# The second norm's shift and scale: columns by one-column products, or by small SBUF-to-SBUF transfers and a sum

## The chip, the cores and the metric

One Trainium2 chip, one of its cores. The metric is device time in microseconds (us) of one launch, median of the runs shown.

## What is computed

One layer of a decoder trunk, 256 tokens of width 1024, float32. Cut to what matters:

```python
mod = silu(c) @ w_ada + b_ada                     # 6 vectors of 1024 from one condition vector
sh1, sc1, g1, sh2, sc2, g2 = split(mod, 6)
h = rms_norm(x, norm1_g) * (1 + sc1) + sh1
ca, cb, q, k, v, gate_conv, gate_attn = split(h @ w_in)
y_conv = conformer_conv(ca, cb, ...)              # 31-tap causal convolution, layer norm, silu, @ w_pw2
y_attn = diff_attention(q, k, v, ...)             # 8 heads, two maps each
merged = sigmoid(gate_conv) * y_conv + sigmoid(gate_attn) * y_attn
x = x + g1 * (merged @ w_out)
h2 = rms_norm(x, norm2_g) * (1 + sc2) + sh2       # sh2, sc2: the vectors of this change
x = x + g2 * moe_ffn(h2, ...)                     # 64 experts, top 8, and one shared
```

## The kernel before

The work has two halves. **The mixer** (to about 337 us): first the modulation of the first norm, then the products of h with w_in in fourteen chunks of 512 columns, two chunks of the convolution's w_pw2 (p0, p1) and two of w_out (o0, o1). Every product is three matmuls on a high and a low part: `splits` casts a weight tile on ACT (L795), `lo_part` subtracts on POOL or VectorE (L776), `products` issues the matmuls (L802 to L804 with tokens as rows, L811 to L813 with channels as rows; the p chunks take the latter, the o chunks the former). Beside this run the convolution `conv` on VectorE (DVE; L859 for the first tap, L863 for thirty more, for eight channel blocks), six units of attention `attn` (scores L1012 and mask L1016, reduce and scale L1023 to L1040, transposes L1046, value products L1057, sub-norm L1069 to L1084), and when the last convolution block is done `layer_norm` (L1102 to L1157), whose result the p products read. Then follow merge, o products, the second norm, routing and ranks. **The experts** (from about 358 us to the end) stream their weights from HBM and multiply.

The modulation's six vectors come in twelve halves of 512; the first four make the first norm's columns in another way. `ada(i)` makes half i for i = 4 to 11: 16 matmuls (L550, in `ada_mm`) leave in a PSUM bank four partial sums, each in 32 equal rows, and ACT copies the bank to a buffer `s` (L742, 128x512). For i = 4, 5, 10, 11 (g1, g2) a matmul with the selector `sel4` (L749) sums the four and spreads the result over all rows. For i = 6, 7 (sh2) and 8, 9 (sc2) the result is wanted as columns, 64 partitions by 8: element c*8+k of the half goes to partition c, column k. Eight products (L758) do that before the change: `s` is the stationary operand, one column of `sel4` the moving one. DVE adds the bias column from PSUM (L762 or L764), and for i = 8, 9 forms the scale (L766).

Nothing in the program text fixes the order of the engines' instructions. Each piece is a generator that announces an engine and a cost in us (`yield "P", 1.0`: 1.0 us of TensorE); the planner `Plan` (L40 to L167) plays all generators at build time, gives each engine to the candidate that can start first and, among those, to the one of highest priority (`PRIO`, L25: attention 8, layer norm 7.5, `ada` 2, the convolution 0), and issues instructions in the order found. A changed cost or step moves all that is planned after it. DMAs on the SP queue (weights) and on ACT's queue are ordered so too.

```python
yield "P", 1.0
for k in range(K):
    nc.tensor.matmul(p[h, k:k + 1], sv[:, k], sel4[:, 0:1], start=True, stop=True)
yield pl.ev("cols")
yield TS(8)
```

Of the kernel before, what the change touches and what calls it, by code (L numbers as in the profile page):

```python
# [14 lines left out]
OP = mybir.AluOpType  # L15
AX = mybir.AxisListType
# [159 lines left out]
def TS(n):  # L176
    return "D", 0.13 + 0.00052 * n
# [10 lines left out]
def AP(n, table=None):  # L188
    return "A", 0.06 + 0.00082 * n, table
# [6 lines left out]
def MM(n):  # L196
    return "P", n / 2400.0
# [3 lines left out]
def tile_hybrid_block(ctx, tc, x, c, positions, w_ada, b_ada, norm1_g, w_in, conv_dw, conv_dw_b,  # L201
# [3 lines left out]
    nc = tc.nc  # L205
    P, T, D, K = 128, 256, 1024, 8
# [6 lines left out]
    pl = Plan()  # L213
# [218 lines left out]
    def done(key, q, now=None):  # L432
        now = pl.cur.ready if now is None else now
        w = loaded[key]
        if w.off[q] in halves:
            e = halves.pop(w.off[q])
            load(*e, [1], now)
            advance(now)
        elif w.off[q] in once:
            once.remove(w.off[q])  # L440
        elif w.off[q] == LAST:
            w2s.close()
            obs = ctx.enter_context(tc.tile_pool(name="obs", bufs=1)).tile([P, 8 * KB], F32R, name="obs")
            pl.put("ob", *(ob_of(obs[:, i * D:(i + 1) * D]) for i in range(2)))
        else:
            pl.pools["w"].append((now, w.off[q]))
            advance(now)
# [17 lines left out]
    sel4 = cst.tile([P, P], F32, name="sel4")  # L465
# [44 lines left out]
    pcol = cst.tile([P, 96], F32, name="pcol")  # L510
    c2 = pcol[:, 65:89].rearrange("p (a k) -> p a k", a=3)
# [21 lines left out]
    for k in range(K):  # L533
        p = B[k // 2][:, (k % 2) * T:(k % 2 + 1) * T]
# [11 lines left out]
    def ada_mm(i, s):  # L546
        w = loaded["a", i].k
        for k in range(K):
            g = k % 4
            nc.tensor.matmul(s[32 * g:32 * g + 32], ccol[:, k:k + 1].to_broadcast([P, 32]), w[k],  # L550
                             start=(k < 4), stop=(k >= 4))
# [10 lines left out]
    h32 = cst.tile([P, 3, 256], F32, name="h32")  # L562
    pl.put("h32", *(h32[:, i] for i in range(3)))
    pl.put("sa", *sa)
    s8_ = cst.tile([P, 4, 3, 8], F32, name="s8")
    pl.put("s8", *(s8_[:, i] for i in range(4)))
    pl.put("t2", *(temp(2 * i, 512) for i in range(3)))
# [155 lines left out]
    p2 = cst.tile([P, K], F32, name="p2")  # L723
    a2c = cst.tile([P, K], F32, name="a2c")
    b2c = cst.tile([P, K], F32, name="b2c")

    def late_ada(i):
        yield from ada(i, "sa")

    def ada(i, pool):  # L730
        yield pl.ev("mod", 3)
        yield pl.ev("L", "a", i, 3)
        yield max(loaded["a", i].at)
        row = i in (4, 5, 10, 11)
        p = yield Get("bank")
        yield "P", 1.8
        ada_mm(i, p)
        for q in range(2):
            done(("a", i), q)
        s = yield Get(pool)  # L740
        yield AP(512)
        nc.scalar.copy(s, p)  # L742
        if row:
            r = brow[i]
            yield pl.ev("param", {4: 3, 5: 4, 10: 11, 11: 12}[i])
            yield "G", 1.25
            nc.gpsimd.tensor_tensor(s[r:r + 1], s[r:r + 1], badar[r:r + 1], op=OP.add)
            yield MM(4 * 512)
            nc.tensor.matmul(p, sel4, s, start=True, stop=True)  # L749
            d = slice((i % 2) * 512, (i % 2) * 512 + 512)  # L750
            yield AP(512)
            nc.scalar.copy((g1b if i < 10 else g2b)[:, d], p)
        else:
            h = slice(64 * (i % 2), 64 * (i % 2) + 64)
            sv = s.rearrange("p (c k) -> p k c", k=K)
            yield "P", 1.0
            for k in range(K):
                nc.tensor.matmul(p[h, k:k + 1], sv[:, k], sel4[:, 0:1], start=True, stop=True)  # L758
            yield pl.ev("cols")
            yield TS(8)  # L760
            if i < 8:
                nc.vector.tensor_tensor(b2c[h], p[h, 0:K], c2[h, 0], op=OP.add)  # L762
            else:
                nc.vector.tensor_tensor(p2[h], p[h, 0:K], c2[h, 1], op=OP.add)  # L764
                yield TS(8)
                nc.vector.scalar_tensor_tensor(a2c[h], p2[h], 1.0, c2[h, 2], op0=OP.add, op1=OP.mult)  # L766
        pl.put("bank", p)
        pl.put(pool, s)
        pl.set("ada", i)

# [1151 lines left out]
    for i in range(4, 10):  # L1922
        pl.spawn(ada(i, "sa"))
# [77 lines left out]
```

## Time and profile before

| | |
|---|---|
| median of 3 runs | 820.47 us (818.65 to 822.19) |
| the profiled execution | 819.49 us, span 817.7 us, mean granted TensorE clock 0.969 |
| busy share of the span | PE 94%, DVE 54%, ACT 40%, POOL 24% |
| HBM | 330 GB/s mean over the span, about 420 GB/s from 358 us on |

PE is TensorE, DVE is VectorE, ACT is ScalarE, POOL is GpSimd, SP is the engine that issues most DMAs; ACTq and POOLq are DMA issues of those engines. A float32 matmul is recorded as two, so that eight products show as 16 records. "PEclk" is the granted clock of TensorE: 1.00 is 2.4 GHz, 0.50 is 1.2 GHz. An [idle <-engine line] behind an instruction is time for which its engine stood idle before it, and what ended the wait.

### The profile page before, as it was taken

How to read it: one execution, taken by the hardware profiler on the slowest of the kernel's cores; microseconds unless marked ns; L12 is line 12 of the kernel's file. 1: busy time of each engine (PE TensorE's matmuls, PEld its weight loads, DVE VectorE, ACT ScalarE, POOL GpSimd, SP SyncE). 2: the span in 40 equal slices, each digit the busy share in tenths (PEclk: the TensorE clock that was granted, in tenths of full speed). 3: DMA queues.
4: the chain of work that ended last, by engine and by line, in shares of the span. 5: the costliest groups of instructions: out<-in, count | busy, mean ns of one | idle time of the engine just before them, and what ended most of it. 6: DMA issues, size and time to landing. Idle time of an engine off the chain costs nothing.

```text
span 817.7 us, 13180 instructions
## 1 busy us (share of the span) xinstructions
PE 766.1 (94%) x4759; PEld 469.8 (57%) x4759; DVE 444.6 (54%) x1035; ACT 324.9 (40%) x713; POOL 192.4 (24%) x246
## 2 busy tenths in 40 slices
PE   3999999899996999999999797999999999999997
PEld 2898777589784987545454141354464455444543
DVE  5458998999996677433433141344344344433443
ACT  4356656865759755223221021232232232232220
POOL 3003788888572693000002000000000000000000
PEclk9999999899997999989999898999999999999999
DMA  9998776546654676469999999999999999999993
GB/s 312 365 336 288 261 253 227 180 161 227 228 184 155 239 280 252 165 245 390 390 420 420 422 421 420 421 422 420 420 421 422 421 420 421 420 421 419 419 413 139
DMA packets 69883, 271.04 MB, mean 331 GB/s; under 512 B 6085, under 2 KB 15893, under 8 KB 46520
## 3 DMA queue, kind: packets, MB, share of 16 engines
q1 hardware_dynamic: 69464, 270.00, 84.9%
q8 instruction: 38, 0.62, 0.3%
q0 software_dynamic: 304, 0.16, 0.1%
q14 instruction: 29, 0.24, 0.1%
q10 hardware_dynamic: 48, 0.01, 0.0%
HBM read 269.11 MB, written 1.05 MB: 330 GB/s over the span
## 4 chain that ended last, share of the span: by engine, by line


## 5 line engine op out<-in xcount | busy, mean ns | idle before, releaser
L1802 PE MATMUL bank<-fa 128*32 128x512 f32 (+2 forms) x1048 | 203.7, 608 | 8.3 <-DMA fa<-in_w_exp_gu_dram 8.3
L1802 PEld LDWEIGHTS bank<-fa 128*32 128x32 f32 (+2 forms) x1048 | 60.3, 124 | 132.1 <-issue 107.3
L863 DVE SCALAR_TENSOR_TENSOR bank<-fa,tap,bank 128x256 f32<-128x256 f32 x232 | 112.9, 486 | 6.1
L1676 DVE SCALAR_TENSOR_TENSOR fa<-bank,gsc,h 128x256 f32<-128x256 f32 x28 | 13.5, 484 | 170.1 <-ACT h L1672 170.1
L1849 PE MATMUL bank<-fa 128*32 128x512 f32 (+1 forms) x496 | 83.9, 596 | 0.0
L1672 ACT ACTIVATE h<-bank 128x256 f32<-128x256 f32 x28 | 10.8, 385 | 179.7 <-PE bank L1802 179.7
L776 POOL TENSOR_TENSOR rb<-fa,rb 128x512 fp32r<-128x512 f32 x46 | 60.2, 1317 | 65.6 <-ACT rb L795 64.6
L1694 DVE TENSOR_TENSOR fa<-bank,fa 128x512 f32<-128x512 f32 x54 | 37.4, 692 | 65.5 <-PE bank L1849 62.7
L776 POOL TENSOR_TENSOR ra<-fa,ra 128x512 fp32r<-128x512 f32 x48 | 63.9, 1339 | 20.5 <-ACT ra L795 17.1
L1762 ACT CAST obs<-fa 128x512 fp32r<-128x512 f32 x54 | 33.4, 618 | 83.7 <-DVE fa L1694 83.7
L1719 DVE TENSOR_TENSOR fa<-fa,bank 128x512 f32<-128x512 f32 x108 | 66.7, 678 | 0.0
L1491 ACT ACTIVATE fa<-bank,b2c,a2c 128x256 f32<-128x256 f32 x108 | 53.6, 561 | 20.8 <-PE bank L1523 20.8
L795 ACT CAST ra<-fa 128x512 fp32r<-128x512 f32 x76 | 46.8, 622 | 37.0 <-PE bank L812 22.9
L1523 PE MATMUL bank<-ra 128*128 128x256 f32 x448 | 60.5, 288 | 0.0
L1710 PE MATMUL bank<-obs,ra 128*128 128x512 f32 x216 | 58.3, 412 | 0.0
L795 ACT CAST rb<-fa 128x512 fp32r<-128x512 f32 x68 | 42.0, 623 | 37.8 <-PE bank L812 22.4
L1802 PE MATMUL bank<-late_w,fa 128*32 128x512 f32 (+2 forms) x168 | 51.9, 627 | 4.1 <-DMA late_w<-in_w_exp_gu_dram 4.1
L1523 PEld LDWEIGHTS bank<-ra 128*128 128x128 f32 x448 | 55.6, 191 | 0.2
L1710 PEld LDWEIGHTS bank<-obs,ra 128*128 128x128 f32 x216 | 38.7, 188 | 28.8 <-issue 21.5
L811 PE MATMUL bank<-ra 128*128 128x256 f32 x160 | 47.8, 299 | 1.9 <-ACT ra L577 1.8
L1849 PEld LDWEIGHTS bank<-fa 128*32 128x32 f32 (+1 forms) x496 | 22.8, 119 | 41.1 <-issue 35.3
L811 PE MATMUL bank<-ra,rb 128*128 128x256 f32 x160 | 46.1, 288 | 0.0
(376 smaller groups left out, 1391.5 us busy)
## 6 DMA issues: line engine op xcount, KB each, us to landing
fa<-in_w_exp_gu_dram SPq DMA_DIRECT2D x100, 1024.0 KB, 19.8
fa<-in_w_exp_down_dram SPq DMA_DIRECT2D x50, 1024.0 KB, 19.8
fa<-in_w_ada_dram SPq DMA_DIRECT2D x24, 1024.0 KB, 7.9
fa<-in_w_in_dram SPq DMA_DIRECT2D x22, 1024.0 KB, 5.3
late_w<-in_w_exp_gu_dram SPq DMA_DIRECT2D x17, 1024.0 KB, 19.3
late_w<-in_w_exp_down_dram SPq DMA_DIRECT2D x12, 1024.0 KB, 6.8
fa<-in_w_exp_gu_dram SPq DMA_DIRECT2D x22, 512.0 KB, 9.4
fa<-in_w_in_dram SPq DMA_DIRECT2D x12, 512.0 KB, 9.4
```

Of the source, the lines that this page charges most:

```text
L776: (nc.gpsimd if e == "G" else nc.vector).tensor_tensor(hl[:, 1], w.k[k], hl[:, 0].bitcast(F32), op=OP.subtract)
L795: nc.scalar.copy(hl[:, 0], w.k[k])
L811: nc.tensor.matmul(o, hl[:, 0, mm], src_t[:, k, 0], start=(k == 0 and m % 2 == 0), stop=False)
L863: nc.vector.scalar_tensor_tensor(cv[:, m] if j == TAPS - 1 else acc, u_sb[:, m, j:j + T], tap[:, m, j:j + 1], acc, op0=OP.mult, op1=OP.add)
L1491: nc.scalar.activation(xt[:, k, 0:ns], p3[:, f2, 0:ns], AF.Identity, bias=b2c[:, k:k + 1], scale=a2c[:, k:k + 1])
L1523: nc.tensor.matmul(p3[:, f2, 0:ns], xr[:, a, t, (f + f2) * P:(f + f2 + 1) * P], tables[b0][:, t, 0:ns], start=(f2 + t + a == 0), stop=(f2 ...
L1694: nc.vector.tensor_tensor(o32, pd[h], g2b[:, h * 512:(h + 1) * 512], op=OP.mult)
L1710: nc.tensor.matmul(p, info.pT[:, t * P:(t + 1) * P], ob[a], start=(a == 0), stop=(a == 1))
L1719: nc.vector.tensor_tensor(x_sb[:, t, d], x_sb[:, t, d], p, op=OP.add)
L1762: nc.scalar.copy(ob[0], o32)
L1802: nc.tensor.matmul(pg[o:o + m], info.xt[:, k, o:o + m], loaded["g", js[e]].k[k], start=(k == 0), stop=(k == K - 1))
L1849: nc.tensor.matmul(pd[h][o:o + m], info.aT[:, f, o:o + m], loaded["d", js[e]].k[f][:, h * 512:(h + 1) * 512], start=(f == 0), stop=(f == 1))
```

## The change

For i = 6 to 9 the products go. Behind ACT's copy of the bank to `s` (L742 before, L744 after) the bank is given back at once; four DMAs from ACT's queue (after: L762) take row 32g of `s`, for g = 0 to 3, one row of 512, and lay each as 64 partitions by 8 into `parts`, a part of the tile `pcol`; DVE sums over the four (L767 TENSOR_REDUCE, 64x8 from 64x8x4), adds the bias (L770), and for i = 8, 9 forms the scale (L774). The plan counts 0.4 us of ACT for the four issues and lets the reduce start 3.0 us after them.

```diff
+    for i in range(2):
+        pl.put(f"acol{i}", pcol[64 * i:64 * i + 64, 0:32].rearrange("p (g k) -> p g k", g=4))
...
             h = slice(64 * (i % 2), 64 * (i % 2) + 64)
-            sv = s.rearrange("p (c k) -> p k c", k=K)
-            yield "P", 1.0
-            for k in range(K):
-                nc.tensor.matmul(p[h, k:k + 1], sv[:, k], sel4[:, 0:1], start=True, stop=True)
+            pl.put("bank", p)
+            p = None
+            parts = yield Get(f"acol{i % 2}")
+            yield "A", 0.4
+            for g in range(4):
+                nc.scalar.dma_start(parts[:, g], s[32 * g:32 * g + 1])
+            yield pl.cur.ready + 3.0
             yield pl.ev("cols")
+            yield TS(32)
+            half = b2c[h] if i < 8 else p2[h]
+            nc.vector.tensor_reduce(half, parts.rearrange("p g k -> p k g"), axis=AX.X, op=OP.add)
+            pl.put(f"acol{i % 2}", parts)
             yield TS(8)
-            if i < 8:
-                nc.vector.tensor_tensor(b2c[h], p[h, 0:K], c2[h, 0], op=OP.add)
-            else:
-                nc.vector.tensor_tensor(p2[h], p[h, 0:K], c2[h, 1], op=OP.add)
+            nc.vector.tensor_tensor(half, half, c2[h, 0 if i < 8 else 1], op=OP.add)
+            if i >= 8:
                 yield TS(8)
                 nc.vector.scalar_tensor_tensor(a2c[h], p2[h], 1.0, c2[h, 2], op0=OP.add, op1=OP.mult)
-        pl.put("bank", p)
+        if row:
+            pl.put("bank", p)
```

The instructions are re-planned between the first group of products (113 us in the trace of before) and the end of the p products (292 us); ahead of that and behind it the engines' orders are the same but for buffer numbers. SP's order of weight loads is the same throughout. In the listings below line numbers of after are those of before plus 2 (up to L744) or plus 8 (from L771 on).

First place, **ACT around the first group**, after, with the semaphores that an instruction waits for. A DMAHW semaphore is one of eight that the hardware DMAs of SP and ACT take in turn, and a DMA waits until the earlier DMA of its semaphore has landed:

```order
106 L918 ACTIVATE s_211<-s_211 128x8 [waits DVE_49]
107 L744 COPY fa<-bank_77 128x512 [waits PE_49]
108 L762 DMA pcol<-fa 64x1x8 [waits DMAHW2_49,Activation_49]
109 L762 DMA pcol<-fa 64x1x8 [waits DMAHW3_49]
110 L762 DMA pcol<-fa 64x1x8 [waits DMAHW4_49]
111 L762 DMA pcol<-fa 64x1x8 [waits DMAHW5_49]
112 L803 CAST rb<-fa 128x512 [waits PE_49,Pool_49]
113 L803 CAST ra<-fa 128x512 [waits PE_49,Pool_49]
```

Four issues stand ahead of casts that feed the products; before, the cast followed the copy directly.

Second place, **DVE at the end of the convolution** (L863 to fa is the last tap; L1110 and L1115 belong to the layer norm, the other lines to attention). Before:

```order
251 L1023 TENSOR_REDUCE mx<-bank_79 128x2
252 L1084 SCALAR_TENSOR_TENSOR fa<-bank_74,sl_213,fa 128x4x128
253 L863 SCALAR_TENSOR_TENSOR bank_77<-fa,tap,bank_77 128x256 x5
254 L863 SCALAR_TENSOR_TENSOR fa<-fa,tap,bank_77 128x256 x2
255 L1110 TENSOR_SCALAR fa<-bank_78 128x256
256 L1115 TENSOR_TENSOR fa<-fa 128x256 x5
257 L1023 TENSOR_REDUCE mx<-bank_74 128x2
258 L1031 RECIPROCAL mx<-mx 128x2x2
```

After:

```order
291 L871 SCALAR_TENSOR_TENSOR bank_74<-fa,tap,bank_74 128x256
292 L1092 SCALAR_TENSOR_TENSOR fa<-bank_75,sl_213,fa 128x2x128
293 L1079 TENSOR_SCALAR mx<-mx 128x2
294 L871 SCALAR_TENSOR_TENSOR bank_74<-fa,tap,bank_74 128x256 x2
295 L1083 TENSOR_TENSOR fa<-bank_75,mx 128x256
296 L871 SCALAR_TENSOR_TENSOR fa<-fa,tap,bank_74 128x256 x2
297 L1031 TENSOR_REDUCE mx<-bank_73 128x2
298 L1092 SCALAR_TENSOR_TENSOR fa<-bank_78,sl_213,fa 128x2x128
299 L1031 TENSOR_REDUCE mx<-bank_76 128x2
300 L1118 TENSOR_SCALAR fa<-bank_80 128x256
```

Attention work that stood behind the last tap has moved ahead of it.

Third place, **PE around the layer norm's last sum (L1138; after, L1146)**, up to the first p product (L819 after; before, three more L1012 and two masks L1016 come first). Before:

```order
1157 L749 MATMUL bank_80<-fa,sel_111 128x512
1158 L1057 MATMUL bank_76<-fa 128x128 x4
1159 L1138 MATMUL bank_78<-fa,ones 128x128 x2
1160 L1046 MATMUL bank_73<-ident,fa 128x128 x4
1161 L1079 MATMUL bank_76<-ident,fa 128x128 x2
1162 L1057 MATMUL bank_73<-fa 128x128 x4
1163 L1012 MATMUL bank_74<-fa 128x256
```

After:

```order
1167 L1136 MATMUL bank_80<-ones,fa 128x1 x2
1168 L1065 MATMUL bank_75<-fa 128x128 x4
1169 L1146 MATMUL bank_80<-fa,ones 128x128 x2
1170 L1087 MATMUL bank_75<-ident,fa 128x128 x2
1171 L819 MATMUL bank_77<-ra 128x256
```

L749, which belongs to the halves 10 and 11, and the attention matmuls behind L1138 but for one L1079 (after: L1087) stand further ahead; so do those that stood among the 192 p products (12 instructions of L1046, L1057 and L1079).

## Rows read from the trace of the kernel before

**Rows 1.** The page: the span, and the busy time of each engine with its share of the span and its instructions.

```profile
span 817.7 us, 13180 instructions
...
PE 766.1 (94%) x4759; PEld 469.8 (57%) x4759; DVE 444.6 (54%) x1035; ACT 324.9 (40%) x713; POOL 192.4 (24%) x246
```

**Rows 2.** Stretches of the span (start:end, length, busy us of PE, PEld, DVE, ACT, POOL each with its number of records, granted clock, DMA share, GB/s): from the first group of products to the end of the convolution, from there to the first p product, the p products, the experts.

```profile
112.00:243.00 131.00, 125.09 (x821) 103.26 (x822) 121.00 (x261) 85.82 (x210) 100.74 (x135) 0.95 0.63 216
243.00:266.00 23.00, 15.36 (x76) 9.57 (x75) 15.79 (x44) 20.30 (x52) 6.98 (x8) 0.78 0.39 139
266.00:292.00 26.00, 25.53 (x212) 25.18 (x211) 15.19 (x29) 18.08 (x39) 19.45 (x17) 1.00 0.65 220
...
358.00:793.00 435.00, 421.06 (x2540) 200.73 (x2538) 160.16 (x346) 110.67 (x237) 5.09 (x4) 0.98 1.01 417
```

**Rows 3.** The instructions of L758: records, ns least/median/most, first and last start; who waited for them (us, times).

```profile
  L758 PE MATMUL bank<-sel,fa x64: 258/258/282, 112.8 to 187.7; 128*64 128x1 f32 x64
...
  DVE b2c L762: 1.4, 1
  DVE p L764: 0.5, 1
```

**Rows 4.** PE's timeline at the first group (start, us, line, operands, idle before): a product ahead of the group, the group, a product behind it.

```profile
111.30 0.40 PE L804 MATMUL bank<-rb,ra 128*128 128x512 f32 x1
...
112.76 2.08 PE L758 MATMUL bank<-sel,fa 128*64 128x1 f32 x16 [1.06 <-ACT fa L742]
...
116.18 0.63 PE L802 MATMUL bank<-ra 128*128 128x512 f32 x1
```

**Rows 5.** Stretches behind the first two groups, columns as in rows 2.

```profile
115.70:119.10 3.40, 3.40 (x9) 2.63 (x8) 3.33 (x11) 2.20 (x8) 2.40 (x8) 0.50 0.66 229
...
136.20:139.60 3.40, 3.40 (x10) 2.62 (x9) 2.11 (x5) 1.23 (x5) 2.79 (x7) 0.50 1.05 393
```

**Rows 6.** DVE's groups from 112 to 243 us: count | busy us, mean ns of one | idle before and its releaser.

```profile
L863 DVE SCALAR_TENSOR_TENSOR bank<-fa,tap,bank 128x256 f32<-128x256 f32 x177 | 86.0, 486 | 4.5
...
L776 DVE TENSOR_TENSOR rb<-fa,rb 128x512 fp32r<-128x512 f32 x5 | 4.8, 966 | 1.2 <-POOL fa L939 1.2
L776 DVE TENSOR_TENSOR ra<-fa,ra 128x512 fp32r<-128x512 f32 x3 | 3.7, 1233 | 0.6 <-ACT ra L795 0.6
```

**Rows 7.** DVE's timeline: the convolution with other work between its taps, and alone.

```profile
163.31 0.43 DVE L863 SCALAR_TENSOR_TENSOR bank<-fa,tap,bank 128x256 f32<-128x256 f32 x1
163.66 0.34 DVE L1040 SCALAR_TENSOR_TENSOR fa<-fa,mx 128x128 f32<-128x128 f32 x1
163.93 0.48 DVE L863 SCALAR_TENSOR_TENSOR bank<-fa,tap,bank 128x256 f32<-128x256 f32 x1
...
176.22 12.55 DVE L863 SCALAR_TENSOR_TENSOR bank<-fa,tap,bank 128x256 f32<-128x256 f32 x24
```

**Rows 8.** DVE's timeline from the last taps on.

```profile
241.90 0.87 DVE L863 SCALAR_TENSOR_TENSOR fa<-fa,tap,bank 128x256 f32<-128x256 f32 x2
...
246.52 0.68 DVE L1023 TENSOR_REDUCE mx<-bank 128x2 f32<-128x512 f32 x1
247.12 0.16 DVE L1031 RECIPROCAL mx<-mx 128x4 f32<-128x4 f32 x1
...
247.51 0.69 DVE L1034 TENSOR_SCALAR mx<-mx,lam 128x2 f32<-128x2 f32 x1
...
254.89 0.48 DVE L1135 TENSOR_SCALAR fa<-ident,lnc 128x128 f32<-128x128 f32 x2 [1.03 <-POOL lnc L1132]
...
258.36 0.42 DVE L1069 TENSOR_REDUCE mx<-fa 128x2 f32<-128x256 f32 x1 [1.47 <-ACT fa L1066]
...
259.21 0.48 DVE L1040 SCALAR_TENSOR_TENSOR fa<-fa,mx 128x256 f32<-128x256 f32 x1
```

**Rows 9.** PE's timeline from the layer norm to the first products of p, and the first product of o.

```profile
254.13 2.08 PE L749 MATMUL bank<-fa,sel 128*128 128x512 f32 x2 [0.46 <-POOL fa L747]
...
257.70 1.06 PE L1138 MATMUL bank<-fa,ones 128*128 128x128 f32 x4
...
263.71 2.08 PE L1012 MATMUL bank<-fa 64*128 64x256 f32 x8
...
265.92 0.36 PE L811 MATMUL bank<-ra 128*128 128x256 f32 x1
...
266.24 0.28 PE L813 MATMUL bank<-ra 128*128 128x256 f32 x1
266.36 0.28 PE L811 MATMUL bank<-ra 128*128 128x256 f32 x1
...
291.57 0.39 PE L802 MATMUL bank<-ra,mt 128*128 128x512 f32 x1
```

**Rows 10.** ACT's timeline at the start of the program: the two DMAs that ACT issues before the change.

```profile
0.74 0.59 ACTq L287 DMA_DIRECT2D fa<-in_c_dram  x1
1.36 0.33 ACTq L462 DMA_DIRECT2D fa<-in_b_ada_dram  x1
```

**Rows 11.** DMA issues: operands, queue, count, KB of one, median us from issue to landing.

```profile
out_dram<-fa SPq DMA_DIRECT2D x2, 256.0 KB, 2.1
...
fa<-in_norm_g_dram POOLq DMA_DIRECT2D x1, 4.0 KB, 5.0
fa<-in_b_ada_dram ACTq DMA_DIRECT2D x1, 8.0 KB, 4.0
```

## The prediction

> **What bounds the kernel now.** I read the page first: PE is busy for 94% of the span, the others for much less [rows 1]. That share mixes two halves. In the experts' half, the stretch table shows a DMA share of 1.01 at 417 GB/s [rows 2]: the weight stream is the limit there and nothing of this change touches it, so a change in the time must come as an earlier or later end of the mixer, passed through unchanged. The removed products lie at 112.8 to 187.7 us, all in the mixer [rows 3]. There the stretch table shows two engines full at once: from 112 to 243 us PE is busy for 125.1 of 131 us and DVE for 121.0 [rows 2]. What counts is which of them sets the end of that stretch. The timeline of DVE answers it: 243 us is the end of the convolution's last tap (241.90 + 0.87 [rows 8]), a chain of accumulating DVE instructions, and the layer norm behind it, on which the p products depend, cannot begin before. In DVE's groups the convolution idles only 4.5 us in 177 instructions [rows 6]. So **DVE leads and PE runs beside it**, close behind; between 243 and 266 us neither is full, PE 15.4 of 23 us [rows 2], and a chain of layer norm and left-over attention sets the time.
>
> **What the change removes.** On PE, four groups of 16 records: 2.08 us each, 8.3 us; PE stood 1.06 us for ACT's copy ahead of the first [rows 4]. Behind the first two groups the granted clock is 0.50 for 3.40 us each [rows 5]; a product of 512 columns takes 0.63 us there instead of 0.40 [rows 4]. At half clock 3.40 us do the work of 1.7, so 3.4 us in all if the products caused it. PE is thus relieved of 8.3 + 1.1 + 3.4 = 12.8 us. That would be the gain if PE led. Since DVE leads, I cost it at nothing, covered by the convolution; if that cover goes, it is a rival's price below. On DVE, the waits for the products go: 1.4 + 0.5 = **-1.9 us** [rows 3]. These stood on the chain of the taps.
>
> **What it adds to DVE directly.** Four reduces and the same number of bias additions as before, 64 partitions by 8: each like the shortest DVE rows, 0.16 us [rows 8]. The new wait is for landings. The trace of before has no SBUF-to-SBUF transfer; the nearest rows are ACT's small one at 4.0 us, POOL's at 5.0, and the quickest landing of all, 2.1 us [rows 11]. Issue of one took ACT 0.33 to 0.59 us [rows 10], so four take 1.3 to 2.4 where the plan has 0.4; copy to last landing is then 3.4 to 6.4 us (to 7.4 with POOL's row), against the plan's 0.4 + 3.0 = 3.4. DVE arrives about when the plan says, so each reduce can stop it for 0 to 3.0 us (4.0 with POOL's), 0 to 12 (16) for four. Behind it in line stand the taps and L776, whose low parts the products on PE wait for; the stop is paid in full while it is no longer than what DVE waits for anyway. I take a quarter, **+3.0 us**, since most transfers have other work in front of the reduce. A gain is excluded here. ACT's own 1.3 to 2.4 us per group delay the casts behind them (the listing of ACT); ACT is busy for 86 of 131 us [rows 2], so I cost this at nothing, up to 1 us per group if PE drains its casts. The DMA semaphores are shared with SP: an issue can stop ACT until an earlier weight load has landed. Nothing of before shows that wait; it belongs to the second rival.
>
> The Trainium skill speaks against the change: its page "DMA: Bandwidth & Descriptors", section "Anatomy of one DMA", gives a fixed cost of about 2.0 us per DMA, written for GpSimd's path, and "Rules for kernel authors" says to coalesce many small transfers. By that price copy to landing is an estimated 3.3 to 4.4 us, DVE's waits are 0 to 4, and the sum below would be -3.1 to +0.9; the rows of other small transfers here lie above it, and no row shows one between two places of SBUF.
>
> **What it moves.** The order shows what the plan makes of it: attention that stood behind the last tap now stands ahead of it. Counted in DVE's order, up to the last tap there are more of L776 (3), L1023 (2), L1040 (4), L1034 (2), L1069 and L1075 (4), L1084 (1), and eight short ones (L1031, L1071 and the new column work). Prices: L776 (4.8 + 3.7) / 8 = 1.06 [rows 6], and from DVE's end stretch 0.68, 0.48, 0.69, 0.42 (L1075 has the shape of L1069), 0.48 (L1084, shape of L1040) and 0.16 [rows 8]: 3.2 + 1.4 + 1.9 + 1.4 + 1.7 + 0.5 + 1.3 = 11.4 us in 24 instructions. But the convolution alone leaves bubbles: 24 taps take 12.55, 0.52 each, while a tap and an L1040 of 0.34 together take 163.93 - 163.31 = 0.62 [rows 7]. An instruction between taps costs its duration less 0.24 us. If all 24 stand singly, 5.6 us; if none gains, 11.4. I take 18 of 24, as the order mostly alternates: **+7.1 us** at the last tap.
>
> The same move empties what follows. From the last tap (242.8) to the first p product it is 23.1 us, and PE goes from an attention group straight into that product [rows 9]. L749 (2.08) in front of L1138 goes, so does the L1012 block in front of the product (265.92 - 263.71 = 2.2 [rows 9]), and two L1023 no longer stand between the layer norm's steps (1.4 [rows 8]): **-5.7 us**; at least 2.1 if only one of these was on the chain, at most 7.2, all from L1138's end at 258.76 to 265.92. The p products themselves take 291.57 - 265.92 = 25.65; 192 at the pitch of 0.12 are 23.0 [rows 9], and the attention between them is gone: **-2.6 us**, or 0 if casts and low parts set that pace (POOL is busy 19.5 of 26 us [rows 2]).
>
> **The sum:** -1.9 + 3.0 + 7.1 - 5.7 - 2.6 = -0.1 us. Against the profiled execution, 819.49, that is 819.4; this execution lies 1.0 us under the median of the runs shown, so I forecast **820.4**. Anything under 0.5%, 4.1 us, cannot be told from no change by a measurement of this kernel.
>
> **Rivals.**
> *DVE absorbs the work* (chance 0.30, faster). DVE is idle 10.0 of the 131 us [rows 2]; PE, 12.8 us lighter, could feed it earlier, and the 11.4 us fall into that idle time, costing 1.4 instead of 7.1. With half the landing waits (1.5): -1.9 + 1.4 + 1.5 - 5.7 - 2.6 = -7.3, so 813.2. For it: PE is as full as DVE in this stretch, and some of DVE's waits are for ACT and POOL, which wait for others. Against: PE receives the moved attention, at least 2.08 + 2.08 + 2.6 = 6.8 us, so it keeps only 6 of its relief; and the idle time in front of taps is mostly the bubbles that I have counted. It decides from 4.0 us less than forecast at the last tap.
>
> *Late landings* (0.18, slower). Each reduce stops DVE, in front of taps and low parts, for as long as a 4.0 us landing behind 2.4 us of issues exceeds the plan: 3.0 us, four times 12, 9 over my term: 829.4; with POOL's 5.0, 833.4. For it: every small transfer of the trace but one lands in 4 us or more, the products' stretch loads weights at up to 1.05 DMA share [rows 5], and the shared semaphores tie some of the sixteen issues to weight loads. Against: the four go out together, and the plan leaves 3.0 us. It decides from 7.2 us of waits in all, 1.8 per group, which is a last landing 5.2 us behind the copy.
>
> *The tail keeps its length* (0.10, slower). Attention was only filling waits of the layer norm; 2.1 comes back instead of 8.3, so 826.6. Against: PE had no idle time just ahead of the first p product [rows 9].
>
> *Nothing passes on* (0.08, no change): the experts' start depends on weights that arrive when they do, and the mixer's few us vanish there: 820.5. Against: the DMA share from 112 to 292 us is 0.39 to 0.65 [rows 2], so the stream has room to follow a mixer that ends earlier or later. Forecast as above: 0.34.
>
> **Numbers.** Faster by over 0.5% 0.30, within 0.42 (0.34 + 0.08), slower 0.28 (0.18 + 0.10). The range takes the first rival down to a little under its price, 811, and the second to a little over its own, 831; 2 in 10 remain outside, for PE's relief passing in full or landings like POOL's.
>
> **What would show it.** Right: no L758, PE's busy time some 8 us less in all, the first 0.50 stretch gone; the last tap some 8 us later than 242.8; from there to the first p product about 17.4 us; the p products 23 us; L767 waiting under 1 us each for a DMA. The second rival shows as waits over 1.8 us in front of each L767, or of ACT's issues. The forecast is wrong if the last tap does not come later, or if the stretch behind it is as long as before.

## The result and the profile after

The changed kernel takes 826.88 us (median, 823.78 to 829.23) against 820.47: a ratio of 1.0067, 95% interval 1.0050 to 1.0085. It is slower, by 0.5 to 0.85%, where no change was forecast.

The page of the changed kernel, span and busy times (as in [rows 1]):

```profile
span 827.0 us, 13075 instructions
...
PE 759.3 (92%) x4695; PEld 463.6 (56%) x4695; DVE 447.9 (54%) x1043; ACT 320.9 (39%) x710; POOL 190.4 (23%) x242
```

PE lost the 64 records of the products and 6.8 us of work, and the span grew by 9.3. What DVE waits for between 112 and 258 us (waiting line, releaser, us in all, times, longest), the answer to [rows 3]:

```profile
DVE p L767 <- DMA pcol<-fa: 5.9, 2, 3.1
DVE b2c L767 <- DMA pcol<-fa: 1.8, 1, 1.8
DVE rb L784 <- ACT rb L803: 1.8, 1, 1.8
```

Landings stop DVE for 7.7 us where the products stopped it for 1.9. The last line is new too: a low part waits for a cast that stands behind the four issues on ACT. The transfers themselves (ns of one issue least/median/most; then us from issue to landing), and ACT's first and last group of four (start, us):

```profile
L762 ACTq DMA_DIRECT2D pcol<-fa x16: 471/608/1461, 113.7 to 179.6; - x16
...
DMA to landing us min/median/max: 4.1/5.5/7.4
```

```profile
113.69 3.64 ACTq L762 DMA_DIRECT2D pcol<-fa  x4
...
177.06 3.18 ACTq L762 DMA_DIRECT2D pcol<-fa  x4
```

So a group costs ACT 2.4 to 3.6 us (the plan has 0.4), and 5.5 us pass until 2 KB have landed. DVE's timeline at the last taps ([rows 8] has them at 241.90), and PE's where the p products and the o products begin and wait ([rows 9]):

```profile
256.26 0.86 DVE L871 SCALAR_TENSOR_TENSOR fa<-fa,tap,bank 128x256 f32<-128x256 f32 x2
```

```profile
272.07 0.58 PE L819 MATMUL bank<-ra 128*128 128x256 f32 x1
273.59 0.58 PE L820 MATMUL bank<-ra 128*128 128x256 f32 x1 [0.94 <-DVE ra L1162]
...
299.01 0.40 PE L810 MATMUL bank<-ra,mt 128*128 128x512 f32 x1
...
307.09 0.51 PE L810 MATMUL bank<-ra,mt 128*128 128x512 f32 x1 [0.96 <-ACT mt L1188]
...
312.55 0.50 PE L812 MATMUL bank<-ra,mt 128*128 128x512 f32 x1 [1.50 <-DVE mt L1190]
```

And the stretches between (columns as in [rows 2]): from the last tap, to the first p product, and the p products in two parts.

```profile
257.10:264.30 7.20, 0.82 (x4) 0.34 (x2) 6.96 (x20) 5.39 (x18) 1.16 (x2) 0.85 0.34 130
264.30:272.10 7.80, 5.60 (x23) 4.39 (x23) 4.88 (x15) 3.72 (x7) 1.87 (x3) 0.50 0.27 72
272.10:279.20 7.10, 6.16 (x29) 5.87 (x28) 5.13 (x12) 5.98 (x15) 1.28 (x1) 0.50 1.01 428
279.20:299.00 19.80, 19.80 (x167) 19.80 (x167) 7.92 (x13) 10.95 (x20) 15.78 (x13) 1.00 0.45 143
```

The stretch behind the last tap did shrink, from 23.2 to 15.0 us, as the order promised. But PE is nearly empty in its first half, the clock is 0.50 when the p products begin, and stays there for 7 us. Stage by stage, read off the traces in the same way for every kernel below (us; first tap = first start of the L863 of that kernel; the mixer ends with the last o product):

| kernel | first tap at | taps | last tap to p | p | o | first tap to mixer's end | median | ratio to before, 95% |
|---|---|---|---|---|---|---|---|---|
| before | 71.7 | 171.1 | 23.2 | 25.7 | 26.0 | 245.8 | 820.5 | 1 |
| changed | 72.9 | 184.2 | 15.0 | 26.9 | 27.5 | 253.6 | 826.9 | 1.0050 to 1.0085 |
| e1, no transfers | 72.9 | 180.8 | 15.0 | 26.9 | 27.5 | 250.1 | 822.9 | 1.0001 to 1.0038 |
| e2, no landing waits | 71.0 | 182.9 | 15.0 | 25.7 | 27.5 | 251.1 | 824.5 | 1.0030 to 1.0065 |
| e3, planned wait 7 us | 71.3 | 183.5 | 16.2 | 26.6 | 27.5 | 253.7 | 825.9 | 1.0031 to 1.0072 |
| e4, before re-planned | 70.9 | 178.2 | 19.9 | 27.2 | 27.5 | 252.8 | 824.0 | 1.0013 to 1.0051 |
| e5, issued by SP | 71.8 | 187.2 | 15.0 | 26.3 | 27.5 | 256.0 | 828.0 | 1.0063 to 1.0113 |
| e8, old order | 70.1 | 192.0 | 23.3 | 25.7 | 26.0 | 267.0 | 837.9 | 1.0174 to 1.0228 |
| e9, late sum, re-planned | 71.5 | 177.9 | 20.3 | 26.3 | 27.5 | 252.0 | 823.2 | 1.0005 to 1.0038 |
| e12, old order, late sum | 72.7 | 169.2 | 23.5 | 26.4 | 26.0 | 245.1 | 817.9 | 0.9948 to 0.9978 |
| e13, as e12, issued by SP | 69.8 | 168.0 | 23.1 | 26.4 | 25.9 | 243.4 | 814.3 | 0.9908 to 0.9951 |
| e14, convolution first | 69.2 | 141.4 | 42.5 | 93.1 | 26.4 | 303.5 | 873.9 | 1.0624 to 1.0672 |

The first tap comes at 69 to 73 us, ahead of anything that the change touches; that is how single executions differ, so stages are compared from there on: the mixer is 7.8 us longer in the changed kernel's profile, the medians are 6.4 apart. Each row of stages is one execution, not a median: that of before lies 1.0 us under its median and e13's 1.1, those of the changed kernel, e1 and e4 lie 2.3, 3.9 and 2.2 above theirs. A stage that differs by 1 or 2 us proves nothing by itself. e11, the probe, has one run, 822.3 us.

### The profile page after: what moved, and what is told of

Read it like the earlier page. It is cut to its first block, busy times and chain, and to the rows that moved or that the text cites. A ratio compares the mean times of both kernels' runs of the same rounds, so it can differ in the third digit from the quotient of the medians.

```text
span 827.0 us, 13075 instructions
## 1 busy us (share of the span) xinstructions
PE 759.3 (92%) x4695; PEld 463.6 (56%) x4695; DVE 447.9 (54%) x1043; ACT 320.9 (39%) x710; POOL 190.4 (23%) x242
## 4 chain that ended last, share of the span: by engine, by line
## 5 line engine op out<-in xcount | busy, mean ns | idle before, releaser
L784 POOL TENSOR_TENSOR rb<-fa,rb 128x512 fp32r<-128x512 f32 x44 | 57.3, 1308 | 79.1 <-ACT rb L803 78.3
L1531 PE MATMUL bank<-ra 128*128 128x256 f32 x448 | 60.5, 288 | 0.0
L819 PE MATMUL bank<-ra 128*128 128x256 f32 x160 | 48.8, 305 | 1.8 <-ACT ra L579 1.8
L820 PE MATMUL bank<-ra 128*128 128x256 f32 x160 | 47.7, 298 | 0.9 <-DVE ra L1162 0.9
L821 PE MATMUL bank<-ra 128*128 128x256 f32 x160 | 47.3, 296 | 0.0
```

Of the source, the lines that this page charges most:

```text
L784: (nc.gpsimd if e == "G" else nc.vector).tensor_tensor(hl[:, 1], w.k[k], hl[:, 0].bitcast(F32), op=OP.subtract)
L819: nc.tensor.matmul(o, hl[:, 0, mm], src_t[:, k, 0], start=(k == 0 and m % 2 == 0), stop=False)
L820: nc.tensor.matmul(o, hl[:, 0, mm], src_t[:, k, 1], start=False, stop=False)
L821: nc.tensor.matmul(o, hl[:, 1, mm], src_t[:, k, 0], start=False, stop=last)
L1531: nc.tensor.matmul(p3[:, f2, 0:ns], xr[:, a, t, (f + f2) * P:(f + f2 + 1) * P], tables[b0][:, t, 0:ns], start=(f2 + t + a == 0), stop=(f2 ...
```

## Experiments

Two theories are put against each other: **waits** (what the transfers make DVE and ACT wait for is the loss) and **order** (the new order is the loss).

**e1 and e2: the changed kernel's order, without the transfers, and without waiting for them.** In e1 the issue line is `pass`; in both the reduce reads zeros:

```diff
-            nc.vector.tensor_reduce(half, parts.rearrange("p g k -> p k g"), axis=AX.X, op=OP.add)
+            nc.vector.tensor_reduce(half, u_sb[h, 0:4, 0:8].rearrange("p g k -> p k g"), axis=AX.X, op=OP.add)
```

> The changed kernel with the sixteen transfers left out; the four reduces read columns of zeros that are there from the start, so the second norm has neither shift nor scale. The order on every engine is that of the changed kernel. Waits theory (the loss is what the transfers make DVE and ACT wait): DVE's 7.7 us in front of the reduces and the 1.8 us in front of the first late L784 go, the last tap of the convolution ends at 247 to 249 us instead of 257, and the time is 817 to 820, no slower than before. Order theory (the loss is the attention work that the plan puts ahead of the last tap): the last tap stays at 254 or later and the time at 824 to 828.

> The changed kernel with its transfers issued as they are, but the four reduces read columns of zeros and so wait for no landing (the second norm has neither shift nor scale). Order as in the changed kernel. If DVE's landing waits are the loss: last tap at about 249 us, time 818 to 821. If it is ACT's 11 us of issue time (casts late, low parts late): last tap at 255 or later, time 825 to 828, while the kernel without transfers comes down to 818 to 820. Order theory: 824 to 828 in both.

e1 takes 822.9, e2 824.5: by the medians the transfers cost 4.0 us, 2.4 by the landing waits and 1.6 by ACT's issues (from the first tap to the mixer's end 2.5 and 1.0), and both expectations of the waits theory are missed. The split between the two parts is rough, since each kernel's runs spread over 4 us or more, and a second norm without shift and scale can route tokens to other experts, which the medians include and the mixer does not. Without any transfer the order is still no better than before (1.0001 to 1.0038), and the taps take 180.8 us, 9.7 more than before. Neither theory alone holds.

**e8: the order of before, transfers in the products' place**, reduce and sum under the old addition's plan step.

```diff
             yield "P", 1.0
-            for k in range(K):
-                nc.tensor.matmul(p[h, k:k + 1], sv[:, k], sel4[:, 0:1], start=True, stop=True)
+            for g in range(4):
+                nc.scalar.dma_start(parts[:, g], s[32 * g:32 * g + 1])
```

> The kernel before with its own order on all engines, but each group of eight products replaced at its place by the four transfers, the reduce and the sum (bank given back where it was). Waits theory: with nothing planned for the landing each reduce waits copy-to-landing in full, 2.5 us of issues and 5.5 us, less the 1 to 2 us that DVE has before it: 5 to 7 us a group, last tap at 262 to 270 instead of 243, time 832 to 845. Order theory (transfers cheap, order dear): 818 to 823.

As the waits theory has it: 837.9. Its waits on DVE:

```profile
DVE b2c L762 <- DMA pcol<-fa: 11.8, 2, 6.0
DVE p L762 <- DMA pcol<-fa: 11.5, 2, 5.9
```

23.3 us of waits, and taps and mixer longer by 21: in this order a DVE wait between taps passes in full to the mixer's end. That also shows that DVE leads.

**e4: before with the products planned at 2.1 us instead of 1.0**, one number.

```diff
-            yield "P", 1.0
+            yield "P", 2.1
```

> The kernel before with its products, but their planned cost 2.1 us instead of 1.0, which is what they take. Only the order changes. Waits theory: within 3 us of before, 817 to 824. Order theory (a re-plan alone moves the time by as much as the change did): below 816 or above 824.

824.0, on the edge between the two expectations, and slower than before (1.0013 to 1.0051) with no transfer at all: the o products take 27.5 us as in the changed kernel, and the taps 7.1 more. A re-plan alone costs about half of what the change did.

**e12: the order of before, four landing places, and the sums behind the layer norm** (in `after_norm`, from the list `owed`), where no tap stands behind them.

```diff
+            parts = land[h] if i >= 8 else pcol[h, 0:32].rearrange("p (g k) -> p g k", g=4)
+            for g in range(4):
+                nc.scalar.dma_start(parts[:, g], s[32 * g:32 * g + 1])
...
+            owed.append((i, h, parts))
```

> The kernel before with its own order on all engines; each group of products is replaced at its place by the four transfers on ACT's queue, into four landing places of their own, and the reduces, sums and scales come only behind the layer norm, where nothing waits for them. So PE is relieved of all products, DVE waits for no landing, and the order of the tail is the old one. If PE's relief is worth nothing because DVE leads: last tap at 240.5 to 243, time 818 to 821. If ACT's 10 us of issues hold up the casts: last tap at 244 or later, 822 to 826. If PE led after all: last tap at 238 or earlier, time under 816.

817.9, faster than before (0.9948 to 0.9978), with the last tap at 241.9 us: the case in which DVE leads, 0.1 us under the time expected for it. These are the same transfers, taken out of DVE's way. PE's relief of 12.8 us shows as 1.8 us of the taps.

**e13: e12 with SP issuing** (`nc.sync.dma_start`).

> As the kernel with the old order and the late sum (817.9), but SP issues the sixteen transfers instead of ACT. If ACT's 10 us of issues still cost there: 815 to 817. If they lay in ACT's idle time: 817 to 819. If SP, standing for a copy on ACT, brings weight loads late: 820 or more.

814.3, ratio 0.9908 to 0.9951: the fastest of all, and under every expectation. The taps take 168.0 us, 3.1 less than before, although landings are no quicker (the issues of eight of the sixteen, then all landings):

```profile
236.98 0.87 DVE L861 SCALAR_TENSOR_TENSOR fa<-fa,tap,bank 128x256 f32<-128x256 f32 x2
```

```profile
L759 SPq DMA_DIRECT2D pcol<-fa x8: 464/591/727, 110.7 to 132.4; - x8
...
DMA to landing us min/median/max: 4.2/6.2/9.9
```

**e15: as e12 without transfers.**

> As the kernel with the old order and the late sum, but without any transfer; the late reduces read zeros, so the second norm has neither shift nor scale. It bounds what taking the products off PE can bring in the old order: 815 to 818. If it equals the one with transfers (817.9) within 1.5 us, the transfers themselves cost nothing there and all their price in the changed kernel is the early sum and the new order.

Its total, 1191, says nothing: by the time of the late reduces the columns were no longer zeros (the layer norm uses their place for its squares), the routing changed and the overflow loop ran (the trace has its matmuls from 820 us on). Up to there its stages are those of e13: taps 167.9, mixer 243.4. So in e13 the sixteen transfers cost nothing in the mixer, and all that taking the products away gains there in the old order is 2.4 us.

**e9: the changed kernel with the sums planned behind the layer norm**, so that the plan is made anew; landing places as in e12.

```diff
-            yield pl.cur.ready + 3.0
+            pl.put(pool, s)
+            yield pl.ev("ln", K - 1)
```

> The changed kernel with four landing places and the reduces, sums and scales planned only behind the layer norm; the plan is made anew with that, and orders attention as it likes. Waits theory with what the kernel without transfers showed (waits and issues 4 us, of which the landing waits 2, the rest of the loss in the order): last tap at 249 to 253, 820 to 824, not below before. If the column work and its waits were the whole loss: 815 to 819, faster than before.

823.2, as the waits theory corrected by e1 had it. DVE waits for no landing, and it is still slower than before. Against e12, 817.9, that is the price of the order: 5.3 us.

**e3: only the planned wait, 7.0 us instead of 3.0.**

```diff
-            yield pl.cur.ready + 3.0
+            yield pl.cur.ready + 7.0
```

> The changed kernel with one number changed, the planned wait from issue to reduce, 7.0 us instead of 3.0; landings of 5.5 us are then covered, and the plan is made anew. If the too short wait was the fault: DVE's landing waits under 1 us in all, time 817 to 820. If a new order again costs what it did in the other re-planned kernels: no landing waits, but 821 to 825, o products 27.5 us instead of 26.0.

No landing wait is left, and it takes 825.9, a little over the second expectation: the too short wait was not the fault by itself.

**e5: the changed kernel with SP issuing.**

> The changed kernel, order on PE, DVE, ACT and POOL as it is, but the sixteen transfers are issued by SP, between its weight loads. ACT is then free of 11 us of issues, which the kernel with issues but no landing waits showed to be worth about 2 us: 823.5 to 826. If SP stands waiting for a weight buffer when a transfer is due: landings later, DVE waits over 8 us in all, 827 or more.

828.0, the second expectation, and not better than with ACT: the first reduce now waits 4.2 us (two others 4.2 together; landing up to 8.8). The queue that helps where no tap waits does not help where DVE does.

**e14: the convolution ahead of attention** (`"conv": 8.5` for `"conv": 0`).

> The changed kernel with the convolution's priority above attention's (8.5 instead of 0), re-planned: the taps then run ahead and attention's DVE work falls behind the last tap. If the last tap sets the end: last tap under 235 and time under 818. If DVE's whole work in the mixer counts and the tail only takes what the taps gave: 819 to 826. If products starve because their low parts and PE's attention come late: over 826.

873.9, the third expectation: the taps take 141.4 us, and the stage of the p products 93. The stretches of the taps and of the p stage (columns as in [rows 2]):

```profile
69.20:210.60 141.40, 73.10 (x336) 49.57 (x335) 130.78 (x270) 43.21 (x90) 66.70 (x79) 0.72 0.44 151
...
253.10:346.20 93.10, 91.11 (x751) 83.79 (x750) 52.69 (x85) 71.78 (x168) 65.35 (x61) 1.00 0.70 250
```

While DVE runs the taps, PE is busy for 73.1 of 141.4 us; in the p stage it is full, with 751 matmul records where the p products are 192, and DVE is not. The early last tap alone is worth nothing, because the work that PE was short of comes due behind it.

**e11: a probe in the kernel before.** Two sorts of small extra additions among the taps:

```diff
+                    if j in (4, 9, 14, 19, 24) and m == m0:
+                        nc.vector.tensor_tensor(dum[:, 0], pcol[0:64, 65:73], pcol[0:64, 73:81], op=OP.add)
+                    if j in (4, 9, 14, 19, 24) and m > m0:
+                        nc.vector.tensor_tensor(dum[:, 1], acc[0:64, 0:8], pcol[0:64, 73:81], op=OP.add)
```

> The kernel before with forty small extra DVE additions of 64x8 among the taps, twenty that read and write SBUF only and twenty that read the convolution's PSUM bank; nothing else is changed. If a small SBUF-only DVE instruction is held until the running POOL instruction ends (as starts and ends of the long ones in the trace without transfers suggest), the SBUF-only ones spread from 0.1 to 1.3 us with a mean of 0.4 to 0.7, and the PSUM ones stay at 0.15 to 0.25. If the long ones only had to do with their own inputs: both sorts at 0.15 to 0.25.

The groups of the probe (busy us, mean ns of one | idle before):

```profile
L867 DVE TENSOR_TENSOR dum<-pcol 64x8 f32<-64x8 f32 x20 | 8.9, 446 | 0.0
L869 DVE TENSOR_TENSOR dum<-bank,pcol 64x8 f32<-64x8 f32 x20 | 3.1, 157 | 0.7
```

The same addition takes 157 ns with one operand in PSUM (157 to 160 in all twenty) and 446 on average with both in SBUF (148 to 1133). Twelve of these twenty end 17 to 25 ns after the end of a POOL instruction that ran beside them. The other eight take 148 to 153 ns; five of them met no POOL instruction, and one ran wholly beside a POOL instruction of attention (L1078) without being held. In e1, DVE's and POOL's timelines around the last reduce stand so:

```profile
175.54 1.26 DVE L1048 SCALAR_TENSOR_TENSOR fa<-fa,mx 128x128 f32<-128x128 f32 x1
...
180.09 0.87 DVE L770 TENSOR_TENSOR p<-p,pcol 64x8 f32<-64x8 f32 x1
...
181.51 0.86 DVE L773 SCALAR_TENSOR_TENSOR a2c<-p,pcol 64x8 f32<-64x8 f32 x1
```

```profile
175.37 1.28 POOL L784 TENSOR_TENSOR rb<-fa,rb 128x512 fp32r<-128x512 f32 x1
...
179.64 1.30 POOL L784 TENSOR_TENSOR ra<-fa,ra 128x512 fp32r<-128x512 f32 x1
181.06 1.28 POOL L936 TENSOR_TENSOR fa<-fa,qkg 128x512 f32<-128x512 f32 x1
```

Each of the three DVE instructions ends within 0.15 us of a POOL instruction's end (176.80 and 176.65, 180.96 and 180.94, 182.37 and 182.34). So a short DVE instruction with its operands in SBUF that meets a running POOL instruction is held until that ends, in all cases here but the one named, and the hold is booked as its duration, not as a wait. The Trainium skill, page "SBUF — State Buffer", section "SBUF: two separate sides", has it as an exclusive lock on a port pair that a DVE instruction with two SBUF inputs and a GpSimd one that reads SBUF cannot hold together; the trace agrees, with the 446 against the 157 ns, but for the one instruction named. In the kernel before, the column addition (L762, L764) read the PSUM bank and took 158 and 164 ns on average; in the changed one it reads SBUF only and takes 103 to 729.

## Why the prediction was wrong, step by step

- **DVE leads, PE's relief is worth little: right.** e12 and e15 take PE's 12.8 us away and leave the order alone; the taps shorten by 1.8 and 3.1 us. The -1.9 for the waits that go was a fair price, on the low side. The stretches at half clock that I laid to the products are gone with them: the changed kernel's clock is 1.00 from 27 to 152 us (columns as in [rows 2]). But e4 keeps the products and has one such stretch there, not two (133.2 to 136.6 us), so not every group makes one.

```profile
27.00:152.00 125.00, 121.35 (x801) 95.51 (x789) 99.10 (x221) 72.59 (x153) 64.94 (x85) 1.00 0.84 287
```

- **The landing waits, +3.0: this step failed.** A quarter of the range of 12 was taken on the ground that other work stands in front of the reduce. DVE waited 7.7 us, nearly two thirds of it, three times out of four, since issue (2.4 to 3.6 us a group) and landing (5.5) were both at or beyond the upper ends of the bounds. The bounds came from rows of the program's start and end. The same list of DMAs had small ones that SP issued between its weight loads, 1 to 32 KB at medians of 6.8 to 8.7 us; one of them was issued at 116.4 us, in the stretch of the first products:

```profile
rbias<-in_router_bias_dram SPq DMA_DIRECT2D x1, 32.0 KB, 8.7
```

  This is the second rival, whose point of decision, 7.2 us of waits in all, was passed. ACT's issues, costed at nothing, were worth 1.6 us by the medians of e1 and e2, and 4.1 between the last taps of e12 and e13 (of which 2.9 lie ahead of the first tap, so 1.2).
- **The moved DVE work, +7.1: near in the changed kernel, but with the wrong durations.** From first to last tap DVE is busy 8.5 us longer (159.2 to 167.7) and idle 4.7 longer (11.8 to 16.5). That is the whole of the 13.1 measured, against 8.2 forecast: 7.1 of work and 1.1 of waits. So most of the miss at the last tap, 3.6 of 4.9 us, is idle time. But durations from rows of the tail, where POOL is mostly idle, are not those between the taps, where POOL's low parts hold DVE. Without the transfers' waits (e1) the taps take 12.8 us longer than in e15, where I had 7.1. In e1 the same 360 DVE instructions as in the changed kernel keep DVE busy for 172.8 us instead of 167.7, so taking out the 9.5 us that DVE waited for transfers and the late cast gives back only 3.4. In both kernels every one of these instructions that takes over 0.1 us more than the quick ones of its line and shape (the quickest twentieth over the kept traces) runs beside a POOL instruction (31 in the changed kernel, 35 in e1); of the 75 and 67 that run beside none, not one does. The groups of DVE's attention scaling and of q's and k's norm in e13 and e1 show it (count | busy us, mean ns):

```profile
L1038 DVE SCALAR_TENSOR_TENSOR fa<-fa,mx 128x128 f32<-128x128 f32 (+1 forms) x10 | 5.6, 558 | 0.0
...
L904 DVE TENSOR_SCALAR s<-s 128x8 f32<-128x8 f32 x8 | 3.8, 476 | 0.0
```

```profile
L1048 DVE SCALAR_TENSOR_TENSOR fa<-fa,mx 128x128 f32<-128x128 f32 (+1 forms) x14 | 8.5, 606 | 0.0
...
L914 DVE TENSOR_SCALAR s<-s 128x8 f32<-128x8 f32 x8 | 5.9, 732 | 0.0
```

  The eight TENSOR_SCALARs of the norm are the same in both and cost 2.1 us more.
- **The shorter tail, -5.7: right in kind, and larger,** -8.2 (23.2 to 15.0), also past the 7.2 that I called the most: that bound counted only what lay behind L1138.
- **The p products, -2.6: this step failed as well.** They take 1.3 us more, not 2.6 less. The steady part runs at the pitch forecast (279.20 to 299.00 at clock 1.00), but the same emptying of the tail that saved 8.2 us left PE 0.82 us of work in 7.2, the clock at 0.50 at the first product, and the first seven microseconds at half pace: 29 products took 7.1 us, 0.94 of it a wait for the layer norm's low part, where the pitch of 0.12 makes 3.5. That PE's idleness made the clock fall is read from the order of the two, not tried. Before, attention ran into the products and they began at 1.00 [rows 2]. In e2, which has the same order and where the clock came back sooner (0.92 in the stretch from 273 to 276 us, where the products began at 268.9), p took 25.7. Half clock is not all that sets p: in e12 and e13 the products begin at full clock and take 26.4, since the late sums (265.1 to 267.9 us on DVE in e12) stand in front of attention's DVE work, for which PE waits 0.6 and 0.5 us.
- **The o products were not in the sum.** They take 1.5 us more in every kernel with a new order but e14 (26.4 against 26.0), and in none with the old; PE waits there for merged channels from ACT and DVE (0.96 and 1.50 us above). Why they are late was not tried.

The sum, from the first tap: +13.1 - 8.2 + 1.3 + 1.5 = +7.7 us (7.8 before rounding), against -0.1. The forecast failed where it took a quarter of a landing range that DVE waited out for nearly two thirds, where it credited the p products with 2.6 us that the emptier tail took back at half clock, and where it left the o products out; the tail's larger gain made up for 2.5 of it. What stays open: e13's median gains 6.6 us and its mixer only 2.4; of the 6.3 us between the two profiled executions, 1.9 lie ahead of the first tap and 2.0 behind the last o product, and nothing here says why. Nor is it shown which moved instruction costs what: each new order is shown to cost 3 to 5 us as a whole, by the medians (e4 against before, e1 and e9 against e12).

## What to carry to other kernels

Where a planner orders the work, a changed cost is two changes: try the new operation in the old order and the new order without the operation, as e12 and e1 do, before believing either. A transfer that replaced a short product paid here only with its consumer far behind it: in the old order the sixteen transfers cost 2.0% with the sum among the taps (e8) and gain 0.4 to 0.7% with the sum behind the layer norm (e12, e13). The late sum alone was not enough: in a new order (e9) it is still 0.2% slower than before. And when work is moved ahead of a leading engine's last instruction, price it with the rows of the stretch that it goes to, not of the one that it leaves.

## What the runs showed of the hardware

- An SBUF-to-SBUF transfer of one row of 512 to 64 partitions by 8 (2 KB) lands 4.1 to 7.4 us after its issue, median 5.5, beside weight loads, and the issue itself takes ACT 0.47 to 1.46 us. The 2.0 us that the Trainium skill's page "DMA: Bandwidth & Descriptors" gives as fixed cost ("Anatomy of one DMA", for another path) is less than half of it.
- A 64x8 addition on DVE costs 157 ns with an operand in PSUM and 446 on average with both in SBUF, among POOL's low parts; the held ones end within 25 ns of a POOL instruction's end.
